# One encoder layer on one core: the first squares summed by TensorE, the first norm's factors applied early by ScalarE, a second pair of output tiles without Strassen, and new durations in the planner

## The chip, the core and the metric

The kernel runs on one core of a Trainium2 chip. The core has TensorE (PE, matmuls), VectorE (DVE), ScalarE (ACT), GpSimd (POOL) and SyncE (SP, which here starts nearly all DMAs); each takes its own instructions in order, and they wait for each other through semaphores. In the profile PE stands for matmuls and PEld for the loads of their left operand, which overlap them. The metric is device time of one execution in microseconds (us), the median of 3 runs.

## The reference

One layer of a streaming encoder on 1024 prompt tokens and 32 sample tokens, model width 1024, all in fp32:

```python
x = x + 0.5 * rmsnorm(swiglu(rmsnorm(x, g1a), f1g, f1u, f1d), g1b)
m, ... = mixer(rmsnorm(x, gma), ...)        # attention heads and a gated linear recurrence, side by side
x = x + rmsnorm(m, gmb)
x = x + 0.5 * rmsnorm(swiglu(rmsnorm(x, g2a), f2g, f2u, f2d), g2b)

def rmsnorm(x, g):  return x * rsqrt(mean(x * x, -1) + eps) * g
def swiglu(x, wg, wu, wd):  return (silu(x @ wg) * (x @ wu)) @ wd      # inner width 2816
```

Results are x, the keys and values, and the recurrence's last states.

## The kernel before

Activations lie transposed: the model width on the 128 partitions (8 blocks), the 1056 tokens along the free dimension. The tokens are cut into two sides of 528, and each side into two units of 264; the first feed-forward block takes them as four units. Each fp32 operand is split into a rounded part and a remainder (`split`, a cast on ACT or DVE and a subtraction on DVE), and a product is three matmuls (`mm3`): high by high, high by low, low by high.

`ffn` computes a SwiGLU. Its 22 blocks of inner width are taken as 11 pairs. For pair 0 the products are plain: `natural_products` makes 16 `mm3` for each unit and each of gate and up, so that a unit can start as soon as its own norm is done. From pair 1 on, `products` makes a 2 x 2 x 2 Strassen-like scheme of 7 products of 24 matmuls (168 for gate, 168 for up) in place of 8; it needs sums of blocks of W (`left_operands`) and of X (`right_operands`), which DVE makes, and split casts of them. A product that is added to two outputs is copied out of PSUM by ACT first (`p1`).

A norm is made in three steps: `square_sum` squares each block on ACT (`sq`) and adds it on DVE into `acc`; `rstd` sums `acc` over the partitions with one fp32 matmul for each 128 tokens against a column of ones (`st`), scales it on DVE (`ms`), raises it to -1/2 on POOL, and spreads it over the partitions with three matmuls against the identity (`st` again); then DVE multiplies each block by its gain and by `st` (the scalar_tensor_tensor in `start`'s `end`). In the trace each of these fp32 matmuls of `st` stands as two records.

No order is written by hand. `Planner` records every operation, replays it against a table of durations (`engine_cost`), of delays between engines (`LATENCY`) and of ScalarE's function tables (`TABLES`), tries priorities in several passes, and pins on each engine the order of the best plan; for some casts and copies (`copier`) it also picks the engine, ACT or DVE. So a changed number changes the order in the whole program, and which engine does a cast. After the first feed-forward block come the projections (`pp`), the recurrence (`recur`: matmuls `pg`, sigmoids `ig` and `lx`, tanh and square root in `th`), four attention heads (scores `Sh...`, softmax `P...`, transposes `tps...`, `oh...`), the output projection (`po`) and the second feed-forward block. All records of the trace carry one line, 142, of the planner's `call`, so the rows are told apart by tile names: `pq` for gate and up, `pd` and `pe` for down.

Of the kernel before, what the change touches and what calls it, by code (L numbers as in the profile page):

```python
# [12 lines left out]
F32 = mybir.dt.float32  # L13
# [16 lines left out]
LOUD = 0  # L30
HURRY = 2e4, 0.0, 0.0
# [17 lines left out]
class Planner:  # L49
# [142 lines left out]
    def forward(self, prio):  # L192
# [20 lines left out]
        while todo:  # L213
# [53 lines left out]
            for j, kind in self.after[i]:  # L267
                d = ops[j]
                if kind == ORDER:
                    x = start[i]  # L270
                elif op.size:
                    x = end[i]
                else:
                    x = end[i] + (0 if len(d.engines) == 1 and d.engines[0] == e and (e == "tensor" or kind == AGAIN) else LATENCY[e][d.engines[0]])
                est[j] = max(est[j], x)
                left[j] -= 1
                if not left[j]:
                    release(j)
        return chosen, start, end, order, max(end)

    def backward(self, prio, chosen):
# [12 lines left out]
        while todo:  # L294
# [19 lines left out]
            for j, kind in self.deps[i].items():  # L314
                o = ops[j]
                if kind == ORDER:
                    x = t + cost - o.cost(chosen[j])
                elif o.size:
                    x = t + cost + o.moved + 700 + o.landing
                else:  # L320
                    x = t + cost + (0 if chosen[j] == e and (e == "tensor" or kind == AGAIN) else LATENCY[chosen[j]][e])
# [43 lines left out]
    def pin(self):  # L365

        for row in self.plan.order.values():
# [9 lines left out]
           "vector": {"scalar": 130, "vector": 130, "gpsimd": 180, "sync": 130, "tensor": 256},  # L377
           "scalar": {"scalar": 145, "vector": 145, "gpsimd": 180, "sync": 145, "tensor": 270},
# [3 lines left out]
class Op:  # L382
    def __init__(self, engines, bias, name, args, kw, floor):
# [73 lines left out]
TABLES = {AF.Exp: ("exp",), AF.Tanh: ("exp", "sigmoid"), AF.Sigmoid: ("sigmoid",), AF.Sqrt: ("sqrt",),  # L457
# [3 lines left out]
def engine_cost(engine, op):  # L461
# [4 lines left out]
    if engine == "tensor":  # L466
# [25 lines left out]
def trunk(ctx: ExitStack, tc: tile.TileContext, plan, xt, w1g, w1u, w1d, w2g, w2u, w2d, win, wv, wout, kpast, vpast,  # L492
# [75 lines left out]
    def square_sum(state, src, ring):  # L568
        n = src.shape[2]
        for i in range(src.shape[1]):  # L570
# [24 lines left out]
    def rstd(stat, acc, rest=None):  # L595
        st = stat.stat.tile([128, 512], F32, "st")
        n = acc.shape[1]
# [8 lines left out]
        sums(acc, 504)  # L606
# [19 lines left out]
    def boundary(yp, acc, a, b, res, post_scale, store, then, rest=None):  # L626

        st = rstd(stat, acc, rest)
        for c in range(KD // 2):
# [3 lines left out]
            if rest is not None:  # L633
                for i in range(2):
                    act.activation(y[:, i], y[:, i], AF.Copy, scale=post_scale(2 * c + i))
                dve.tensor_mul(y, y, type(st)(st.tensor, st.offset, [st.ap[0], [0, 2], st.ap[1]]))
            for i in range(2 if rest is None else 0):
# [95 lines left out]

    def products(ps, W, X, out, up_part):


        n = 2
# [43 lines left out]
    def ffn(tails, stat, sides, wg, wu, wd, cuts, finish, last=False):  # L781
# [4 lines left out]
        def gate_up(p):  # L786
            H = [S.tile([128, 2, SB], F32, "H") for _ in range(2)]
            quarters = halves(H[0]) + halves(H[1])
            if p:
                for k, w in enumerate((wg, wu)):  # L790
                    W = left_operands([w[2 * p], w[2 * p + 1]])
                    products(stat.four, W, X, quarters, k)
# [20 lines left out]
            place.close()  # L813
            for s, _, _ in sides:
                X[s] = right_operands(Z[s], X[s])
            return H, quarters
# [121 lines left out]
        place = stat.open(2)  # L938
        for a, b in cuts:
# [6 lines left out]
            for c in range(KD // 2):  # L946
# [3 lines left out]
                for i in range(2):  # L950
# [3 lines left out]
                    if end:  # L954
                        dve.tensor_add(y[:, i], y[:, i], t)
                        square_sum(rest_ if i else acc, y[:, i:i + 1], tp)
                if not end:
                    dve.tensor_add(y, y, q[0][:, :, :b - a])
                    square_sum(acc, y, tp)
            finish(yp, acc[0], a, b, rest_[0])  # L960
# [6 lines left out]
    def start(s):  # L967
# [3 lines left out]
        def part(e):  # L971
# [8 lines left out]

            def end(Z):
# [17 lines left out]
    def finish1(yp, acc, a, b, rest):  # L999
# [5 lines left out]
        def then(c, y):  # L1005
# [3 lines left out]
            square_sum(acc2, y, tp)  # L1009
# [5 lines left out]
    ffn(three, stat, [start(0), start(1)], w1g, w1u, w1d, CUTS1, finish1)  # L1015
# [451 lines left out]
    def mixed(s):  # L1467
# [3 lines left out]
        def part(e):  # L1471
# [6 lines left out]
            def begin(Z):  # L1478
                for c in range(KD // 2):
# [5 lines left out]
                    square_sum(acc, yp(c), tp)  # L1485

            def end(Z):
                def then(c, y):
                    if y is not None:
                        square_sum(acc2, y, up)  # L1490
                        return
                    st = rstd(stat, acc2[0])
                    for c in range(KD // 2):
                        for i in range(2):
                            dve.scalar_tensor_tensor(yp(c)[:, i], yp(c)[:, i], col("g2a", 2 * c + i), st,
                                                     op0=ALU.mult, op1=ALU.mult)
# [8 lines left out]
    def finish2(yp, acc, a, b, rest):  # L1505
        boundary(yp, acc, a, b, x2_d, lambda k: half[:, 8 + k:9 + k],
                 lambda c, a, b: y_o["y%d_o" % a][:, 2 * c:2 * c + 2], lambda c, y: None, rest=rest)

    ffn(three, stat, [mixed(1), mixed(0)], w2g, w2u, w2d, CUTS, finish2, last=True)
# [81 lines left out]
```

## Time and profile before

| | |
|---|---|
| median of 3 runs | 1951.77 us (1951.39 to 1957.23) |
| profiled execution | 1959.79 us, of which the span of the trace is 1958.0 us |
| PE busy | 1897.3 us, 97% |
| DVE, ACT, POOL busy | 1417.7, 656.2, 62.2 us |
| mean granted clock of TensorE | 0.987 |

PE is the busy engine, so that time is lost where PE waits, where it runs at its lower clock, or where it is given more matmuls. Matmul records overlap: one of 264 columns lasts 0.28 us in the trace, but the next starts 0.12 us after it, so that rates are read from counts in a stretch.

### The profile page before, as it was taken

To read this page: it belongs to the slowest core of one execution; us is meant where nothing else is said; L and a number is where in the kernel's file an instruction comes from. 1 tells how busy PE (TensorE), PEld (TensorE's weight loads), DVE (VectorE), ACT (ScalarE), POOL (GpSimd) and SP (SyncE) were. 2 spreads that over 40 slices of the span, in tenths; PEclk is the share of its full clock that TensorE was granted. 3 is DMA by queue.
4 is the path that set the end of the run, shared out by engine and by line. 5 is a ranking of instruction groups with operands and counts; after the bars stand their busy time and mean duration, and the time that the engine had idled before them with its cause. 6 is when DMAs were issued, how large, how long until landed. Compare 5 with 4: busy or idle time off the path is not lost. (4 is left out here: it accounts for less than half of the span.)

```text
span 1958.0 us, 35215 instructions
## 1 busy us (share of the span) xinstructions
PE 1897.3 (97%) x14456; PEld 1853.7 (95%) x14456; DVE 1417.7 (72%) x2612; ACT 656.2 (34%) x1292; POOL 62.2 (3%) x79
## 2 busy tenths in 40 slices
PE   6999999999999999998999899999999999999997
PEld 6999999999999999897988699999999999999997
DVE  8867677675888588348677857987676666687947
ACT  5322122223232053046367753432222221333302
POOL 1000000000000010000100000100000000000000
PEclk9999999999999998999999799999999999999998
DMA  3232333324634254134434432332323323553442
GB/s 133 83 104 83 99 105 105 104 83 145 214 105 149 88 153 133 65 124 123 112 105 113 128 109 84 111 110 83 112 97 110 93 83 99 172 194 122 141 143 89
DMA packets 127810, 225.61 MB, mean 115 GB/s; under 512 B 11424, under 2 KB 84896, under 8 KB 127648
## 3 DMA queue, kind: packets, MB, share of 16 engines
q1 hardware_dynamic: 127504, 223.31, 36.0%
q8 instruction: 113, 1.85, 0.4%
q14 instruction: 49, 0.40, 0.1%
q10 hardware_dynamic: 144, 0.05, 0.0%
HBM read 157.48 MB, written 65.83 MB: 114 GB/s over the span
## 5 line engine op out<-in xcount | busy, mean ns | idle before, releaser
L142 PE MATMUL pq<-X,W 128*128 128x264 f32 x7488 | 926.8, 286 | 11.0 <-ACT p L142 4.7
L142 PEld LDWEIGHTS pq<-X,W 128*128 128x128 f32 x7488 | 921.8, 190 | 12.7 <-ACT p L142 5.1
L142 PE MATMUL pd<-T,W 128*128 128x264 f32 x3024 | 368.6, 284 | 0.0
L142 PEld LDWEIGHTS pd<-T,W 128*128 128x128 f32 x3024 | 368.1, 188 | 0.0
L142 ACT CAST W<-raw 128x512 fp32r<-128x512 f32 (+1 forms) x251 | 147.7, 601 | 433.3 <-PE pq L142 269.7
L142 DVE TENSOR_TENSOR W<-raw,W 128x512 fp32r<-128x512 f32 (+1 forms) x376 | 243.9, 669 | 5.7 <-ACT W L142 2.2
L142 DVE TENSOR_TENSOR u<-p,pq 128x528 f32<-128x528 f32 x80 | 56.3, 703 | 180.4 <-PE pq L142 180.1
L142 PE MATMUL pp<-xm,w 128*128 128x352 f32 x384 | 128.1, 334 | 6.1 <-DVE y L142 2.8
L142 PE MATMUL pp<-xm,wl 128*128 128x352 f32 x384 | 127.0, 332 | 1.9 <-DVE wl L142 1.9
L142 DVE TENSOR_TENSOR raw<-raw 128x512 f32<-128x512 f32 (+1 forms) x150 | 115.0, 771 | 17.0 <-DMA raw<-in_w2d 9.0
L142 DVE TENSOR_TENSOR u<-u,pq 128x528 f32<-128x528 f32 x80 | 56.3, 704 | 48.7 <-PE pq L142 48.4
L142 ACT CAST T<-traw 128x528 fp32r<-128x528 f32 x75 | 45.3, 633 | 118.6 <-DMA traw<-t_d 96.1
L142 DVE TENSOR_TENSOR T<-traw,T 128x528 fp32r<-128x528 f32 x126 | 84.2, 702 | 1.1
L142 PEld LDWEIGHTS pp<-xm,w 128*128 128x128 f32 x384 | 73.6, 192 | 8.3 <-ACT sq L142 3.0
L142 PE MATMUL po<-cat,w 128*128 128x264 f32 x256 | 74.9, 298 | 2.6 <-DVE y L142 1.5
L142 POOL TENSOR_TENSOR ms<-ms,neghalf 128x3 f32<-128x3 f32 x24 | 29.2, 1218 | 1518.1 <-DVE ms L142 1518.1
L142 DVE TENSOR_TENSOR acc<-acc,sq 128x264 f32<-128x264 f32 x167 | 68.9, 426 | 11.4 <-ACT sq L142 9.6
L142 PEld LDWEIGHTS pp<-xm,wl 128*128 128x128 f32 x384 | 73.7, 192 | 3.3 <-DVE wl L142 2.8
L142 PE MATMUL po<-cat,wl 128*128 128x264 f32 x256 | 72.7, 290 | 1.6 <-DVE wl L142 0.9
L142 PE MATMUL pe<-h,w 128*128 128x264 f32 x256 | 73.3, 287 | 0.0
L142 PE MATMUL pe<-hl,w 128*128 128x264 f32 x256 | 72.9, 285 | 0.0
L142 PE MATMUL pe<-h,wl 128*128 128x264 f32 x256 | 72.7, 286 | 0.0
(408 smaller groups left out, 2531.6 us busy)
## 6 DMA issues: line engine op xcount, KB each, us to landing
t_d<-H SPq DMA_DIRECT2D x126, 264.0 KB, 2.2
traw<-t_d SPq DMA_DIRECT2D x56, 528.0 KB, 4.5
raw<-in_w1g SPq DMA_DIRECT2D x22, 512.0 KB, 3.6
raw<-in_w1u SPq DMA_DIRECT2D x22, 512.0 KB, 4.1
raw<-in_w2g SPq DMA_DIRECT2D x22, 512.0 KB, 3.6
raw<-in_w2u SPq DMA_DIRECT2D x22, 512.0 KB, 3.9
raw<-in_w1d SPq DMA_DIRECT2D x36, 256.0 KB, 4.4
raw<-in_w2d SPq DMA_DIRECT2D x36, 256.0 KB, 4.3
```

The costliest lines, as they stand in the source:

```text
L142: self.made.append(f(*args, **kw).ins)
```

## The change

Four things. (1) For units 0 and 1 of the first norm (`MATRIX`), ACT squares two blocks in one instruction, and PE sums the squares over blocks and partitions: 24 fp32 matmuls of one column for each unit in place of 3, and no adds on DVE. (2) In all four units of the first norm (`SCALED`), ACT multiplies each block by its gain before the norm's factor is known (32 activations), and DVE then multiplies by `st` two blocks at a time (16 tensor_tensor in place of 32 scalar_tensor_tensor). (3) In the first feed-forward block (`PLAIN` 2) pair 1 is plain as well, by `natural_quarters`: 192 matmuls for gate and 192 for up in place of 168 and 168, and X's sums come after it. The second feed-forward block is as it was (`PLAIN` 1), and so is the end of the program (`early` holds there where `rest` was given before). (4) The planner's numbers:

```diff
-           "vector": {... "tensor": 256},
-           "scalar": {... "tensor": 270},
+           "vector": {... "tensor": 140},
+           "scalar": {... "tensor": 155},
...
+        self.tail = 280 * (name == "matmul" and self.reads[1].dtype == F32)
...
-TABLES = {AF.Exp: ("exp",), AF.Tanh: ("exp", "sigmoid"), ...
+TABLES = {AF.Exp: ("exp",), AF.Tanh: ("exp",), ...
...
-        return max(n * 4 / 2.4, 215)
+        return max(n * 2 / 2.4, 112)
...
+        if name == "tensor_tensor_scan":
+            return 69 + 2 * n / 0.96
```

The code of the other three:

```diff
+PLAIN = 2, 1
+MATRIX = "start0", "start1"
+SCALED = "start",
...
+    class Matrix:
+        def __init__(self, stat, n):
+            self.st, self.n, self.begun = stat.stat.tile([128, 512], F32, "st"), n, False
+
+        def add(self, sq):
+            for i in range(sq.shape[1]):
+                for j, a in enumerate(range(0, self.n, 128)):
+                    b = min(a + 128, self.n)
+                    pe.matmul(self.st[:, 504 + j:505 + j], sq[:, i, b - 128:b], ones[:, 0:1], start=not self.begun,
+                              stop=True, skip_group_check=True)
+                    self.begun = True
...
+    def square_sum(state, src, ring, where=None, stat=None):
         n = src.shape[2]
+        if where in MATRIX:
+            if state[0] is None:
+                state[0] = Matrix(stat, n)
...
+                sq = ring.tile([128, src.shape[1], n], F32, "sq")
+                act.activation(sq, src, AF.Square)
+                state[0].add(sq)
+            return
...
+    def scaled(ys, g, st, early):
+        if early:
+            for c, y in enumerate(ys):
+                for i in range(2):
+                    act.activation(y[:, i], y[:, i], AF.Copy, scale=g(2 * c + i))
+            st = st()
+            for y in ys:
+                dve.tensor_mul(y, y, twice(st))
+            return
...
+    def natural_quarters(ps, W, X, out, up_part):
+        for r in range(2):
+            for e in range(2):
+                t = ps.tile([128, 2, 512], F32, "pq")
+                for s in range(2):
+                    for h in range(2):
+                        for kk in range(4):
+                            a, b = X[s][h, e][kk // 2], kk % 2
+                            mm3(t[:, s, :HB], W[r, h], cslice(kk), (a[0][:, b], a[1][:, b]), slice(0, HB),
+                                h == kk == 0, h == 1 and kk == 3)
...
             if p:
                 for k, w in enumerate((wg, wu)):
-                    W = left_operands([w[2 * p], w[2 * p + 1]])
-                    products(stat.four, W, X, quarters, k)
+                    W = left_operands([w[2 * p], w[2 * p + 1]], p < plain)
+                    (natural_quarters if p < plain else products)(stat.four, W, X, quarters, k)
+                    if k and p == plain - 1:
+                        sums()
...
                 for c in range(KD // 2):
-                    square_sum(acc, z[c], tp)
-                st = rstd(stat, acc[0])
-                for c in range(KD // 2):
-                    for i in range(2):
-                        dve.scalar_tensor_tensor(z[c][:, i], z[c][:, i], col("g1a", 2 * c + i), st, op0=ALU.mult, op1=ALU.mult)
+                    square_sum(acc, z[c], up if mark in MATRIX else tp, mark, stat)
+                scaled(z, lambda k: col("g1a", k), lambda: rstd(stat, acc[0]), "start" in SCALED)
```

What the planner makes of it stands in the order of each engine. PE's first instructions, before (`st` is the norm's tile, `pq` the first products, `X` a split unit, `W` a split weight):

```order
L142 MATMUL st_450<-ones_344,acc_427 128x1 x3
L142 MATMUL st_450<-ident_348,ms_451 128x128 x2
L142 MATMUL st_450<-ident_348,ms_451 128x8
L142 MATMUL pq_480<-X_468,W_373 128x264
L142 MATMUL pq_531<-X_468,W_389 128x264
L142 MATMUL pq_480<-X_468,W_373 128x264 x5
L142 MATMUL pq_480<-X_471,W_373 128x264
L142 MATMUL st_609<-ones_344,acc_586 128x1 x3
```

and now:

```order
L145 MATMUL st_427<-ones_344,sq_444 128x1 x6
L145 MATMUL st_427<-ones_344,sq_452 128x1 x6
L145 MATMUL st_427<-ident_348,ms_468 128x128 x2
L145 MATMUL st_427<-ident_348,ms_468 128x8
L145 MATMUL st_596<-ones_344,sq_597 128x1 x6
L145 MATMUL st_596<-ones_344,sq_605 128x1 x6
L145 MATMUL st_596<-ones_344,sq_613 128x1 x6
L145 MATMUL st_596<-ones_344,sq_621 128x1 x6
L145 MATMUL pq_490<-X_478,W_373 128x264
L145 MATMUL pq_541<-X_478,W_389 128x264
L145 MATMUL pq_490<-X_478,W_373 128x264 x5
L145 MATMUL pq_490<-X_481,W_373 128x264 x2
```

All 24 sums of unit 0 (the last 12 are shown) and all 24 of unit 1 now stand ahead of the first product; before, three of unit 0 did.

ACT's instructions between the recurrence and the first head's softmax, before (`th` is first a tanh, and from itself a square root; `a2` are squares; `P` are the exponentials of head 0):

```order
L142 ACT_TABLE_LOAD
L142 ACTIVATE th_9467<-th_9467 128x1060
L142 ACTIVATE a2_9745<-lx_8641 128x352
L142 ACTIVATE th_9528<-th_9528 128x1060
L142 CAST w_10052<-raw_10051 128x1024
L142 ACTIVATE th_9650<-th_9650 128x1060
L142 ACTIVATE th_9589<-th_9589 128x1060
L142 ACT_TABLE_LOAD
L142 ACTIVATE P0h0s_10014,sm_10008<-P0h0s_10014,mn_10007 32x544
```

and now:

```order
L145 ACT_TABLE_LOAD
L145 ACTIVATE th_9499<-th_9499 128x1060
L145 ACTIVATE a2_9754<-lx_8667 128x354
L145 ACTIVATE a2_9767<-lx_8670 128x352
L145 ACT_TABLE_LOAD
L145 ACTIVATE th_9682<-lx_8673,sp8_8646 128x1060
L145 ACTIVATE lx_8673<-lx_8673,sp8_8646 128x1060
L145 ACT_TABLE_LOAD
L145 ACTIVATE th_9560<-th_9560 128x1060
L145 ACT_TABLE_LOAD
L145 ACTIVATE P0h0s_10046,sm_10040<-P0h0s_10046,mn_10039 32x544
```

The four square roots stood together and now alternate with the last tanh and the first exponentials, with a table load at each turn; two of them follow later, behind head 0's first exponentials. In the whole program ACT has 40 table loads, 33 before.

## Rows read from the trace of the kernel before

**Rows 1.** Page, busy time of PE, PEld, DVE, ACT and POOL.

```profile
PE 1897.3 (97%) x14456; PEld 1853.7 (95%) x14456; DVE 1417.7 (72%) x2612; ACT 656.2 (34%) x1292; POOL 62.2 (3%) x79
```

**Rows 2.** What PE waited for, whole program: total us, times, longest.

```profile
PE st L142 <- DVE acc L142: 9.3, 2, 9.1
PE st L142 <- POOL ms L142: 6.6, 4, 2.5
```

**Rows 3.** Timeline of PE, 8.9 to 110: start, length, instructions, wait ahead.

```profile
9.09 1.44 PE L142 MATMUL st<-ones,acc 128*128 128x1 f32 x6 [9.09 <-DVE acc L142]
13.05 1.45 PE L142 MATMUL st<-ident,ms 128*128 128x128 f32 x6 [2.52 <-POOL ms L142]
16.14 0.81 PE L142 MATMUL pq<-X,W 128*128 128x264 f32 x2 [1.65 <-ACT X L142]
19.41 1.69 PE L142 MATMUL pq<-X,W 128*128 128x264 f32 x6 [2.46 <-DVE X L142]
...
22.09 1.89 PE L142 MATMUL pq<-X,W 128*128 128x264 f32 x7
...
26.54 3.87 PE L142 MATMUL pq<-X,W 128*128 128x264 f32 x16
...
34.15 0.79 PE L142 MATMUL pq<-X,W 128*128 128x264 f32 x2
...
35.87 13.13 PE L142 MATMUL pq<-X,W 128*128 128x264 f32 x93
49.53 35.40 PE L142 MATMUL pq<-X,W 128*128 128x264 f32 x287 [0.53 <-DVE W L142]
87.19 22.99 PE L142 MATMUL pq<-X,W 128*128 128x264 f32 x174 [2.26 <-ACT p L142]
```

**Rows 4.** Timeline of PEld around the second unit's sums.

```profile
20.79 1.35 PEld L142 LDWEIGHTS st<-ones,acc 128*128 128x128 f32 x6
22.02 1.21 PEld L142 LDWEIGHTS pq<-X,W 128*128 128x128 f32 x5
```

**Rows 5.** Windows: stretch, length, PE busy and count, granted clock, DMA share, GB/s.

```profile
38.00:39.00 1.00, 1.00 (x6) 1.00 0.00 0
...
40.00:41.00 1.00, 1.00 (x11) 1.00 0.00 0
...
88.00:89.00 1.00, 1.00 (x7) 0.50 0.06 16
```

**Rows 6.** Windows: busy and count of PE, PEld, DVE, ACT, POOL; clock, DMA share.

```profile
20.00:30.00 10.00, 10.00 (x47) 9.71 (x45) 10.00 (x28) 6.85 (x17) 0.97 (x1) 1.00 0.01 4
...
905.00:935.00 30.00, 25.06 (x138) 21.34 (x136) 29.07 (x47) 13.37 (x22) 6.23 (x8) 0.94 0.36 113
...
1085.00:1125.00 40.00, 32.96 (x152) 24.93 (x151) 35.23 (x84) 28.48 (x68) 4.26 (x5) 0.74 0.41 130
```

**Rows 7.** Timeline of all engines, 0 to 20.

```profile
3.99 0.42 ACT L142 ACTIVATE acc<-x 128x264 f32<-128x264 f32 x1 [0.20 <-DMA x<-in_xt]
...
8.27 0.62 ACT L142 CAST W<-raw 128x512 fp32r<-128x512 f32 x1 [0.45 <-DMA raw<-in_w1g]
...
15.46 0.63 ACT L142 CAST X<-x 128x528 fp32r<-128x528 f32 x1 [1.03 <-DVE x L142]
```

**Rows 8.** The chain that ended last, in order of time: start, length, what.

```profile
1301.22 284.19 PE pq L142 x2319
```

**Rows 9.** Groups of DVE, 835 to 1245: busy us, mean ns, idle before.

```profile
L142 DVE CAST K<-raw 128x1056 fp32r<-128x1056 f32 x6 | 4.3, 708 | 0.5 <-DMA raw<-k_d 0.5
L142 DVE COPY pth1q<-tpsh1q 128x512 f32<-128x512 f32 x4 | 2.6, 681 | 0.0
```

**Rows 10.** Timeline of ACT in the recurrence.

```profile
862.64 1.17 ACT L142 ACTIVATE th<-lx,sp 128x1060 f32<-128x1060 f32 x1
863.83 1.28 ACT L142 ACT_TABLE_LOAD   x1
865.13 1.19 ACT L142 ACTIVATE lx<-lx,sp 128x1060 f32<-128x1060 f32 x1
```

More of the change, by code (lines that the diff above doesn't have):

```diff
@@ L273, in forward @@
                 else:
-                    x = end[i] + (0 if len(d.engines) == 1 and d.engines[0] == e and (e == "tensor" or kind == AGAIN) else LATENCY[e][d.engines[0]])
+                    x = end[i] + (0 if len(d.engines) == 1 and d.engines[0] == e and (e == "tensor" or kind == AGAIN) else LATENCY[e][d.engines[0]] + op.tail)
                 est[j] = max(est[j], x)
@@ L320, in backward @@
                 else:
-                    x = t + cost + (0 if chosen[j] == e and (e == "tensor" or kind == AGAIN) else LATENCY[chosen[j]][e])
+                    x = t + cost + (0 if chosen[j] == e and (e == "tensor" or kind == AGAIN) else LATENCY[chosen[j]][e] + o.tail)
                 est[j] = max(est[j], x)
@@ L605, in rstd @@
         m = tiny["ms"].tile([128, k])
-        sums(acc, 504)
+        if not known:
+            sums(acc, 504)
         dve.tensor_scalar(m, st[:, 504:504 + k], 1.0 / DM, EPS, op0=ALU.mult, op1=ALU.add)
@@ L624, in block, with twice, boundary @@
         return dram[s, :, 2 * c:2 * c + 2, a - s * SB:b - s * SB]
-    def boundary(yp, acc, a, b, res, post_scale, store, then, rest=None):
+    def scaled(ys, g, st, early):
[7 more added lines that the diff above has]
+            return
+        st = st()
+        for c, y in enumerate(ys):
+            for i in range(2):
+                dve.scalar_tensor_tensor(y[:, i], y[:, i], g(2 * c + i), st, op0=ALU.mult, op1=ALU.mult)
+    def twice(st):
+        return type(st)(st.tensor, st.offset, [st.ap[0], [0, 2], st.ap[1]])
+    def boundary(yp, acc, a, b, res, post_scale, store, then, rest=None, early=False):
         st = rstd(stat, acc, rest)
@@ L632, in boundary @@
             y = yp(c)
-            if rest is not None:
+            if early:
                 for i in range(2):
                     act.activation(y[:, i], y[:, i], AF.Copy, scale=post_scale(2 * c + i))
-                dve.tensor_mul(y, y, type(st)(st.tensor, st.offset, [st.ap[0], [0, 2], st.ap[1]]))
-            for i in range(2 if rest is None else 0):
+                dve.tensor_mul(y, y, twice(st))
+            for i in range(0 if early else 2):
                 dve.scalar_tensor_tensor(y[:, i], y[:, i], post_scale(2 * c + i), st, op0=ALU.mult, op1=ALU.mult)
@@ L732, in natural_products @@
                 act.activation(out[r], t[:, r, :HB], AF.Silu)
+    def natural_quarters(ps, W, X, out, up_part):
[8 more added lines that the diff above has]
+                                h == kk == 0, h == 1 and kk == 3)
+                o = out[2 * r + e]
+                if up_part:
+                    dve.tensor_mul(o, o, t[:, :, :HB])
+                else:
+                    act.activation(o, t[:, :, :HB], AF.Silu)
     def products(ps, W, X, out, up_part):
@@ L813, in gate_up, with sums @@
             place.close()
+            if plain == 1:
+                sums()
+            return H, quarters
+        def sums():
             for s, _, _ in sides:
                 X[s] = right_operands(Z[s], X[s])
-            return H, quarters
         for p in range(FF // 2):
@@ L938, in ffn @@
         place = stat.open(2)
+        mark = "end2" if last else "end1"
         for a, b in cuts:
@@ L955, in ffn @@
                         dve.tensor_add(y[:, i], y[:, i], t)
-                        square_sum(rest_ if i else acc, y[:, i:i + 1], tp)
+                        square_sum(rest_ if i and mark not in MATRIX else acc, y[:, i:i + 1], tp, mark, stat)
                 if not end:
                     dve.tensor_add(y, y, q[0][:, :, :b - a])
-                    square_sum(acc, y, tp)
-            finish(yp, acc[0], a, b, rest_[0])
+                    square_sum(acc, y, tp, mark, stat)
+            finish(yp, acc[0], a, b, rest_[0], last and (a, b) == cuts[-1])
         place.close()
@@ L997, in trunk, with finish1 @@
     xm, rbs = [], []
-    def finish1(yp, acc, a, b, rest):
+    def finish1(yp, acc, a, b, rest, end):
         if not xm:
@@ L1503, in mixed, with finish2 @@
         return s, tiles, [part(1), part(0)]
-    def finish2(yp, acc, a, b, rest):
+    def finish2(yp, acc, a, b, rest, end):
         boundary(yp, acc, a, b, x2_d, lambda k: half[:, 8 + k:9 + k],
-                 lambda c, a, b: y_o["y%d_o" % a][:, 2 * c:2 * c + 2], lambda c, y: None, rest=rest)
-    ffn(three, stat, [mixed(1), mixed(0)], w2g, w2u, w2d, CUTS, finish2, last=True)
+                 lambda c, a, b: y_o["y%d_o" % a][:, 2 * c:2 * c + 2], lambda c, y: None, rest=rest, early=end)
+    ffn(three, stat, [mixed(1), mixed(0)], w2g, w2u, w2d, CUTS, finish2, PLAIN[1], last=True)
     p3_.close()
```

36 lines of the change are left out of this document (20 added, 16 removed).

## The prediction

> **What bounds the kernel now.** The page comes first: PE is busy 1897.3 of 1958.0 us [rows 1], so PE's matmuls are the length, and what else counts is where PE waits or runs slowly. The list of waits puts the largest at the start: 9.3 us for `acc`, 6.6 us for POOL's `ms` [rows 2]. The timeline of PE says what the start is worth [rows 3]. The sums of unit 0 run at 9.09, its broadcast ends at 14.50, and up to 35.87 PE makes only 2 + 6 + 7 + 16 + 2 = 33 products, in pieces, since DVE delivers the split X piece by piece: from 20 to 30 DVE is busy 10.00 of 10 us [rows 6]. So the first stage is bound by DVE and by the norm's chain, not by PE. Then come 93 products in one piece, 0.53 us of wait, 287, and at 87.19 a wait of 2.26 us for a copy of ACT [rows 3]. In the long middle of a feed-forward block nothing waits: 2319 products take 284.19 us [rows 8], 0.1225 us each.
>
> Of the clock: 16 products from 26.54 take 3.87 us, 0.242 us each [rows 3], and at 38 a microsecond shows 6 matmuls where at 40 it shows 11 [rows 5]. That is the pace of the stretch after the wait at 87.19, where the granted clock is 0.50, the lower of the two levels, 1.2 GHz [rows 5]; at the start the column says 1.00 and the pace says otherwise. The pace rose at about 39.4, some 3.5 us after the unbroken run from 35.87 began.
>
> From 690 to 1310 the waits are small and many. Two stretches stand out: 905 to 935 (PE busy 25.06 of 30 us, clock 0.94) and 1085 to 1125 (32.96 of 40, clock 0.74); DVE is busy 29.07 and 35.23 us in them, ACT 13.37 and 28.48 [rows 6]. There DVE is the limit.
>
> **Part 1, sums by PE.** Unit 0's sums are 24 matmuls in place of 3, 48 records. Six records of loads take 22.02 - 20.79 = 1.23 us [rows 4], 0.205 each, so 48 take 9.8 us at the lower level. The first x is there at 3.99 [rows 7]; a square of 528 costs ACT about the 0.63 us of its cast of that size [rows 7], so PE begins near 4.8. The fourth x now has a weight load ahead of it in SP's queue. It lands at the latest when the first weight did, 8.27 [rows 7], long before PE gets to it, so PE itself is the limit: 4.8 + 9.8 = 14.6. From the end of the sums at 10.53 to the end of the broadcast at 14.50 were 4.0 us [rows 3]; `ms` finds DVE idle now, so I take 3.6: 18.2. The order puts unit 1's 24 sums next, 9.8 us more: first product at 28.0, where before it stood at 16.14. By then DVE, free of 14 adds and with 16 wider multiplications for 32, has split all of unit 0, so that PE no longer waits: 9 products at 0.242 (30.2), unit 1's broadcast (1.4, to 31.6), and an unbroken run. I let the clock rise 3.5 to 6.9 us later (the run from 26.54 lasted 3.87 us without a rise), 36.5 in the middle; 20 products fit before. The 67 others of unit 0 take 8.2 us at 0.1225, and the four groups of `st` of units 2 and 3 that are still to come about 0.6 each, half of 1.23: 47.1 us with 96 products done.
>
> **Part 2, factors on ACT.** 32 activations of 264 at 0.42 [rows 7] are 13.4 us more for ACT in the first 60 us. They lie beside PE's sums (ACT is busy 6.85 of 10 us from 20 to 30 [rows 6]) and I cost them at nothing. If the cover is gone, the Silu that frees the first PSUM bank comes late: up to 2 us.
>
> **Part 3, pair 1 plain.** 48 products more, 48 x 0.1225 = 5.9 us. It takes away the copy `p` and the sums of X that crowd DVE at the turn from pair 0 to 1. So the wait at 87.19 goes, and with it the slow stretch behind it: 2.26 us, and 3.4 us at half pace, 1.7; 4.0 together. What is late next would be the split W of pair 2; DVE then has all of pair 1, some 47 us of PE, for about 20 us of X's sums, so I expect no wait there.
>
> The balance at the end of pair 1. Before: 126 products done at 49.53, 594 left at 0.1225, plus 4.0: 126.3. After: 47.1 + (288 + 384) x 0.1225 = 129.4. So the first two parts nearly break even (PE's sums eat what DVE gives back) and the whole is +3.1 us, from +1 (rise of the clock at once) to +6 (late rise and a bank's wait).
>
> **Part 4, the new order of the middle.** No row shows it. By the order, DVE loses between 835 and 1245 two casts of K (0.708 each), three wide copies (0.681) [rows 9] and several smaller things, about 4.9 us together, which go to ACT; 7 table loads of 1.28 us [rows 10] come to ACT, 9.0 us. Bounds: if every wait and slow stretch of the two spots went, 29 us gained (4.94 + 1.8 and 7.04 + 10.4, by [rows 6], is 24.2, the rest smaller waits of 5); if PE stood for each new table load, 9.0 us lost. I take -3.5: seven tenths of the 4.9, since DVE is the full engine where PE waits, and none of the table loads, since ACT has room. The first feed-forward block's other pairs, its down products and the second block have the same work in nearly the same order: 0. The numbers of the planner themselves cost nothing at run time.
>
> The Trainium skill speaks against this part: ScalarE: Activation LUTs, section "What ACT_TABLE_LOAD costs", adds a drain to each load and puts a switch at 2.66 us. By that, 7 switches would be 18.6 us of ACT. The trace disagrees: the load at 863.83 starts 0.02 us after the tanh ended, and the next instruction 0.02 us after the load [rows 10].
>
> **Sum.** 3.1 - 3.5 = -0.4 us. Against the profiled execution (1959.79 us, of which 1.8 lie outside the span) that is 1959.4; that execution was 8.0 us above the median of the runs shown, 1951.77, so the forecast for the median is 1951.4 us. A change under 0.3% (5.9 us) can't be told from none here. The forecast's own range is 1946 to 1957.
>
> **Rivals.**
> A, faster: the new order takes away half of the loss at the two spots. Before, DVE's lateness at the start of a head lets PE wait, and each wait of a few us brings a stretch at the lower clock behind it; 24.2 / 2 = 12.1 us. For it: DVE is full there, and loses work. Against it: the scores still wait for the same K and Q loads and the same softmax. Time 1951.8 + 3.1 - 12.1 = 1942.8.
> B, slower: the table loads stand on the path. The square roots of the recurrence and the first exponentials of head 0 now alternate, so that ACT's exponentials, for which PE's transposes wait, come behind loads and tanh; the 4.9 us taken from DVE come to ACT as well. It decides from about 4 of the 7 loads waited for: 5.1 us, and no gain. Time 1951.8 + 3.1 + 5.1 = 1960.0. For it: ACT is already busy 28.48 of 40 us at the later spot [rows 6]. Against: ACT idles half of the earlier one.
> C, the sums lift the clock. If PE's continuous sums counted as work for the clock, the second 24 would run at half the time (4.9 us less) and the first 29 products too (29 x 0.12 = 3.5): -8.4, 1943.0. Against it stands the trace: from 20 to 30 PE was busy 10.00 of 10 us [rows 6], sums and broadcasts among the products, and the pace stayed low. It is the rule of the Trainium skill's TensorE: Matmul & The Clock Gate, section "What's actually happening", which ties the level to how busy the engine has lately been; by that rule, read plainly, C should happen, and the trace does not bear it out.
>
> **Chances and range.** Forecast 0.50; A 0.21; B 0.20; C 0.05; the rest 0.04, split. Faster by over 0.3% comes from A and C and half the crumbs, 0.27; slower from B, 0.21; within 0.3% 0.52. The range takes in B and nearly all of A and C, with the bounds of the start: 1941 to 1961.
>
> **What would show it.** In the new profile: 48 records of sums ending near 14.6 at 0.2 us each; first product near 28, not before 25 (C would show it near 23); pace 0.12 from about 36; no wait of PE between 32 and 126; the end of pair 1 near 129. If PE stands at the start of pair 2, part 3 is wrong. In the middle: fewer waits for DVE in the windows that answer to 905 to 935 and 1085 to 1125 (A), or waits for ACT's `P` and `th` (B). A first product before 20, or a loss of more than 10 us in the middle, would make the whole argument wrong.

## The result and the profile after

The changed kernel takes 1964.8 us (median of 5 executions, 1962.6 to 1968.8), the kernel before 1954.7 (5 executions, 1951.4 to 1957.2): a ratio of 1.0059 with a 95% interval of 1.0048 to 1.0071, slower by 10 us by the medians, by 11.5 by the ratio. The prediction was 1951.4, with a range from 1941 to 1961; the time lies above it. Its base was low too: in the 20 to 33 executions that stand beside each later run, the kernel before has a median of 1954.7 to 1956.3, not 1951.8.

A second trace of before was taken (`before_again`, below), since the first one's execution (1959.8) was unusually long; what follows compares with the second (1955.0). The page of the changed kernel, the row that answers to [rows 1]:

```profile
PE 1912.4 (97%) x14588; PEld 1870.1 (95%) x14588; DVE 1390.9 (71%) x2546; ACT 682.8 (35%) x1327; POOL 50.9 (3%) x79
```

PE has 132 records more (84 of sums, 48 of products), DVE 66 instructions fewer. The start, timeline of PE of the changed kernel, against [rows 3]:

```profile
5.19 10.40 PE L145 MATMUL st<-ones,sq 128*128 128x1 f32 x48 [5.19 <-ACT sq L145]
16.89 1.45 PE L145 MATMUL st<-ident,ms 128*128 128x128 f32 x6 [1.30 <-POOL ms L145]
18.20 10.38 PE L145 MATMUL st<-ones,sq 128*128 128x1 f32 x48
28.44 2.33 PE L145 MATMUL pq<-X,W 128*128 128x264 f32 x9
30.56 1.28 PE L145 MATMUL st<-ident,ms 128*128 128x128 f32 x6
31.70 6.11 PE L145 MATMUL pq<-X,W 128*128 128x264 f32 x39
...
46.95 13.24 PE L145 MATMUL pq<-X,W 128*128 128x264 f32 x107
```

and the same kernel in windows, where the pace doubles, and over the turns of the first pairs:

```profile
33.00:34.00 1.00, 1.00 (x6) 1.00 (x6) 1.00 (x3) 1.00 (x4) 0.00 (x0) 1.00 0.00 0
34.00:35.00 1.00, 1.00 (x10) 1.00 (x9) 1.00 (x3) 1.00 (x3) 0.00 (x0) 1.00 0.00 0
...
30.00:120.00 90.00, 90.00 (x727) 90.00 (x727) 64.34 (x120) 28.49 (x60) 2.58 (x3) 1.00 0.11 37
```

The start is as forecast: two blocks of 48 records, the first product at 28.4, and no wait of PE in 90 us, where the first trace of before has one of 2.26 us at 87 [rows 3]. Now the marks of the program: first and last start of the down products `pd` of the two blocks, and last `pp` of the projections, first in the second trace of before, then in the changed kernel (count: least/median/longest ns, first to last start):

```profile
L142 PE MATMUL pd<-T,W x1512: 278/284/292, 490.2 to 688.8; 128*128 128x264 f32 x189
L142 PE MATMUL pp<-xm,wl x384: 317/323/662, 735.8 to 1080.4; 128*128 128x352 f32 x192
L142 PE MATMUL pd<-T,W x1512: 278/284/293, 1700.8 to 1887.3; 128*128 128x264 f32 x189
```

```profile
L145 PE MATMUL pd<-T,W x1512: 278/284/391, 494.1 to 693.2; 128*128 128x264 f32 x189
L145 PE MATMUL pp<-xm,wl x384: 317/323/659, 740.1 to 1080.4; 128*128 128x352 f32 x192
L145 PE MATMUL pd<-T,W x1512: 278/284/296, 1708.7 to 1895.4; 128*128 128x264 f32 x189
```

The changed kernel makes the last `pd` of the first block 4.4 us late (688.8 to 693.2), has made all of it good at the last projection (1080.4 both), and then loses 7.9 us before the second block's down products (1700.8 to 1708.7). The spans differ by 8.5. So between these two traces the loss opens far behind the code that was changed; what that is worth, the experiments have to show. The windows show the place; second trace of before, then the changed kernel:

```profile
690.00:1085.00 395.00, 381.02 (x2298) 351.87 (x2296) 281.69 (x609) 198.84 (x401) 34.39 (x49) 0.98 0.40 119
1085.00:1200.00 115.00, 105.85 (x747) 96.13 (x746) 82.65 (x187) 68.06 (x178) 8.97 (x9) 0.96 0.37 122
1200.00:1330.00 130.00, 124.06 (x997) 122.35 (x996) 112.55 (x229) 50.97 (x105) 8.70 (x7) 0.99 0.29 87
```

```profile
690.00:1085.00 395.00, 382.34 (x2331) 352.29 (x2330) 282.13 (x607) 211.76 (x415) 25.73 (x49) 0.99 0.40 119
1085.00:1200.00 115.00, 107.29 (x744) 97.59 (x745) 83.78 (x188) 68.17 (x179) 8.73 (x9) 0.94 0.35 120
1200.00:1330.00 130.00, 119.66 (x939) 118.62 (x938) 110.89 (x227) 47.02 (x101) 7.19 (x7) 0.95 0.28 85
```

From 1200 to 1330 PE makes 939 matmuls where it made 997; 58 at 0.1225 us are 7.1 us. Who it waits for there, in the changed kernel, and the first of these waits in the timeline of PE:

```profile
PE st L145 <- DVE acc L145: 4.4, 1, 4.4
PE pq L145 <- ACT p L145: 2.8, 1, 2.8
PE pq L145 <- ACT X L145: 2.6, 1, 2.6
```

```profile
1212.70 0.28 PE L145 MATMUL po<-cat,wl 128*128 128x264 f32 x1
1217.35 1.41 PE L145 MATMUL st<-ones,acc 128*128 128x1 f32 x6 [4.36 <-DVE acc L145]
```

and DVE of the changed kernel in that time:

```profile
1212.18 0.43 DVE L145 TENSOR_TENSOR acc<-acc,sq 128x264 f32<-128x264 f32 x1
1212.52 0.71 DVE L145 TENSOR_TENSOR y<-y,r 128x528 f32<-128x528 f32 x1
1213.14 0.43 DVE L145 TENSOR_TENSOR acc<-acc,sq 128x264 f32<-128x264 f32 x1
...
1216.77 0.43 DVE L145 TENSOR_TENSOR acc<-acc,sq 128x264 f32<-128x264 f32 x1
```

PE came to the sums of a norm at about 1213, when DVE had made two of that norm's seven adds (the second at 1212.18) and did the others in turn with other work, the last at 1216.77; the products of `po` behind the sums, which follow at once when the sums are through, stood in the queue. The wait and the lower clock behind it (0.95 in place of 0.99 over the stretch) cost the 4.4 us and more: from 1217 to 1222 the granted clock is 0.50, the lower level. No line of this code was changed, but the planner's duration for these sums was. The long chain of [rows 8] then runs as before, 2.7 us later than in the first trace and 7.6 later than in the second (1296.35):

```profile
1303.94 283.95 PE pq L145 x2317
```

### The profile page after: what moved, and what is told of

It reads as the page before. It is cut to its first block, busy times and chain, and to the rows that moved or that the text cites. A ratio compares the mean times of both kernels' runs of the same rounds, so it can differ in the third digit from the quotient of the medians.

```text
span 1961.7 us, 35448 instructions
## 1 busy us (share of the span) xinstructions
PE 1912.4 (97%) x14588; PEld 1870.1 (95%) x14588; DVE 1390.9 (71%) x2546; ACT 682.8 (35%) x1327; POOL 50.9 (3%) x79
## 4 chain that ended last, share of the span: by engine, by line
PE 91%; DVE 4%; DMA 2%; ACT 1%; issue 1%; SPq 0%; POOLq 0%; POOL 0%; DVEq 0%; ACTq 0%
PE pq L145 45%; PE pd L145 19%; PE pp L145 8%; PE pe L145 5%; PE po L145 4%; PE pv L145 3%; PE st L145 3%; DVE y L145 1%; PE Sh1q L145 1%; PE oh2q L145 0%; PE pg L145 0%; PE Sh3q L145 0%; DVE W L145 0%; PE Sh2q L145 0%; DVE wl L145 0%
## 5 line engine op out<-in xcount | busy, mean ns | idle before, releaser
L145 ACT CAST W<-raw 128x512 fp32r<-128x512 f32 (+1 forms) x256 | 151.7, 603 | 393.5 <-PE pq L145 246.1
L145 ACT CAST T<-traw 128x528 fp32r<-128x528 f32 x85 | 51.9, 635 | 137.7 <-DMA traw<-t_d 102.6
L145 DVE TENSOR_TENSOR u<-u,pq 128x528 f32<-128x528 f32 x76 | 53.5, 704 | 46.3 <-PE pq L145 45.5
L145 DVE CAST W<-raw 128x512 fp32r<-128x512 f32 (+1 forms) x116 | 48.6, 424 | 35.0 <-PE pq L145 15.8
L145 DVE TENSOR_TENSOR acc<-acc,sq 128x264 f32<-128x264 f32 x153 | 63.9, 429 | 11.9 <-ACT sq L145 10.6
```

Source lines behind the costliest of these rows:

```text
L145: self.made.append(f(*args, **kw).ins)
```

## The experiments

T1 was the theory that the code of the first stage is the loss; T2, that the new planner numbers make a worse order in the middle and at the turn to the second block; T3, that any new order of this program is worth some us either way, whatever made it. All times are medians with the kernel before on the same chip, all ratios against it with a 95% interval.

**The kernel before, traced again** (no edit).

> The kernel before, profiled once more. The changed kernel is 10 us slower by the medians (1964.8 against 1954.7), but only 3.7 us by the two traces, since the profiled execution of before (1959.8) lay above all its others. Theory T1 (the loss is made by the start and the plain pair and is in the traces as +3.1 at the end of pair 1; the rest is the execution that happened to be profiled): this trace ends near 1951 to 1953, and what it is shorter by is spread over the program. Theory T2 (a stage with DMA waits is now longer or shorter by chance): the difference of the two traces of before sits in one stage, the middle from 690 to 1310.

1955.0 us, span 1953.2: 4.8 us shorter than the first trace. Of these, 1.5 lie before the last `pd` of the first block and 3.3 between there and the first `pd` of the second. So a single trace of this kernel is uncertain by some us, and the first was a long one. (In this expectation T1 and T2 stand for two other theories, which it states itself; the time is above the 1951 to 1953 of the first, and the difference isn't in one stage, as the second has it.)

**The code without the numbers.**

```diff
-"tensor": 140}, "tensor": 155}        (vector, scalar)
+"tensor": 256}, "tensor": 270}
-self.tail = 280 * (...)
+self.tail = 0
-AF.Tanh: ("exp",)
+AF.Tanh: ("exp", "sigmoid")
-return max(n * 2 / 2.4, 112)
+return max(n * 4 / 2.4, 215)
-if name == "tensor_tensor_scan": return 69 + 2 * n / 0.96
```

> Sums by PE, factors on ACT and the plain pair 1, but with the planner's numbers of before. T1 (the code of the first stage is the loss): 1962 to 1966, as the changed kernel, with the end of pair 1 some 3 us late. T2 (the new numbers make a worse order in the middle and at the turn to the second block): 1955 to 1959, only the 3 us of the first stage. T3 (any new order of this program differs by several us either way): anything from 1950 to 1968, with waits at other places than in the changed kernel.

1964.3 us, 1.0046 (1.0032 to 1.0060). The time is T1's, but the way there is another: the last `pd` of the first block comes at 704.0, not 693.5, since PE stands 4.89 us in the first pair and then runs at the lower level (granted clock 0.50 from 75 to 79). PE, then ACT, of this kernel:

```profile
75.12 0.59 PE L145 MATMUL pq<-X,W 128*128 128x264 f32 x1 [4.89 <-ACT H L145]
```

```profile
73.87 0.63 ACT L145 CAST X<-x 128x528 fp32r<-128x528 f32 x1 [19.86 <-DVE W L145]
74.41 0.67 ACT L145 ACTIVATE H<-pq 128x264 f32<-128x264 f32 x2
```

A cast of X stands ahead of the Silu that frees PSUM, and waits for DVE; PE waits for the Silu. Later stages give all of it back against the changed kernel: 382.7 us from that `pd` to the last `pp` against 387.3, and 621.7 from there to the first `pd` of the second block against 628.0.

**The numbers without the code.**

```diff
-PLAIN = 2, 1;  MATRIX = "start0", "start1";  SCALED = "start",
+PLAIN = 1, 1;  MATRIX = ();  SCALED = ()
```

> The code of before with the planner's new numbers (latencies, matmul cost and tail, tanh's table, scan). T1: within 2 us of before, 1953 to 1957. T2: slower by 6 to 8 us, 1961 to 1963, with the waits of the turn to the second block (4.4 us for acc, 2.6 for X, 2.8 for p in the changed kernel). T3: anything from 1950 to 1968.

1954.6 us, 0.9993 (0.9981 to 1.0006). T2's 6 to 8 us are not there: in this order the numbers alone move nothing that can be measured. By the spread of the orders below, one order is weak evidence on an effect of that size.

**The changed kernel with the old start** (`MATRIX = ()`, `SCALED = ()`).

> The changed kernel without sums by PE and without the factors on ACT: plain pair 1 and new numbers stay. By the prediction's parts 1 and 2 the start is even (96 products done at 47.1 against 96 + 30 at 49.5, that is +1.3 us for the sums): 1963 to 1965, the same as the changed kernel within 2 us. If the sums by PE are the loss: 1955 to 1959. T3: anything from 1950 to 1968.

1960.0 us, 1.0023 (1.0014 to 1.0033): between the two expectations. The last `pd` of the first block is at 691.8, 1.7 earlier than in the changed kernel; the rest of the 4.8 us between the medians lies in the later stages.

**The changed kernel with pair 1 as before** (`PLAIN = 1, 1`).

> The changed kernel, but pair 1 by the Strassen-like products as before (sums by PE, factors on ACT and the new numbers stay). Theory P (the 48 more products cost their 5.9 us and what they save, the stall behind pair 0, is worth less): 5.9 us less work and a stall of 2 to 4 us back, as in the kernel with the numbers alone, where PE stands 1.36 + 0.63 + 1.26 us between 56 and 96: 1961 to 1963. If the plain pair pays for itself, as the prediction had it to within 2 us: 1964 to 1967.

1956.1 us, 1.0003 (0.9995 to 1.0012), below both expectations: 8.7 us faster than the changed kernel by the medians, 11 by the ratios, more than the 5.9 us of products that it saves. At the last `pd` of the first block only 3.0 of them are there (690.5 for 693.5). Taken alone, this run would have been read as a price of 8.7 us for the plain pair; that reading doesn't hold, as the next runs show.

**The changed kernel with DVE's adds, factors still on ACT** (`MATRIX = ()`).

> The changed kernel, but with the squares of units 0 and 1 added by DVE as before; factors on ACT, plain pair 1 and new numbers stay. Without both parts the time was 1960.0. Theory M (the 48 matmuls of one column, 20.8 us of PE at the start, are the start's cost): 1958 to 1961, the 96th product near 42.4. Theory S (the factors on ACT are the cost, since ACT is late with the rest): 1963 to 1966, the 96th product near 45.

1960.5 us, 1.0021 (1.0013 to 1.0030). The time is Theory M's, but the way there is neither theory's: the 96th product ends at 36.6 us, before both 42.4 and 45, and 9.3 us are then lost in two waits for `H`, the first for a Silu of ACT, with the lower level between and behind them (0.50 from 72 to 77):

```profile
66.14 1.47 PE L145 MATMUL pq<-X,W 128*128 128x264 f32 x5 [4.77 <-ACT H L145]
72.12 3.23 PE L145 MATMUL pq<-X,W 128*128 128x264 f32 x13 [4.51 <-DVE H L145]
```

The last `pd` of the first block is at 692.0, where the changed kernel has 693.5, but the two marks can't be compared: 47 of the block's 384 `pe` matmuls start ahead of it here, 96 in each other trace, and 49 at 0.1225 us are 6.0 us. The last `pe` ends at 738.5, in the changed kernel at 734.8, in the one with the old start at 733.9. So with the factors on ACT the sums by PE don't cost time in the first block, they save 3.7 us; the factors alone, against the old start, bring the two waits and 4.6 us. All this is one order of each.

**A number moved by 2 ns.**

```diff
-LATENCY = {"tensor": {"scalar": 200, "vector": 198, ...
+LATENCY = {"tensor": {"scalar": 200, "vector": 200, ...
```

> The kernel before with one number of the planner moved by 2 ns (delay from TensorE to VectorE 198 to 200), which no row could tell, but which makes other orders of all engines. Theory T3 (each new order of the middle and of the turn to the second block is worth some us by itself, either way): off from 1954.7 by 2 us or more, with stage lengths that differ by 2 to 5 us in the projections, heads and turn. Theory T1 (such orders are alike to about 1 us): 1953.5 to 1956.

1951.5 us, 0.9978 (0.9968 to 0.9988): faster than before by more than the interval. T3 is borne out: a number that no row could tell is worth 4 us.

**The numbers without the short delays** (256 and 270 stay; code of before).

> The code of before with the new numbers except the two delays towards TensorE (256 and 270 stay). From the end of po to the first pd of the second block the three kernels with all new numbers took 456.3, 455.8 and 455.9 us, those with the old ones 452.9, 452.8 and 453.3. If the short delays make that loss (X is planned to be ready before it is): 453 in that stretch and 1950 to 1953 in all. If the halved matmul cost makes it: 456 in that stretch and 1953 to 1956 in all.

1953.1 us, 0.9983 (0.9975 to 0.9992). The stretch from `po` to `pd` is 448.2, below both expectations; and the kernel with pair 1 as before, which has the short delays, has 453.4. The delays are not the cause. The wait of 4.37 us for `acc` at 1217 stands here as well, and the last `pd` of the first block is at 693.9, where the numbers with the short delays have 688.4 and the changed kernel 693.5, though the code is that of before.

**Two other draws of the changed kernel** (198 to 200, 198 to 196).

> The changed kernel with the same number of the planner moved by 2 ns as in the nudged kernel before (TensorE to VectorE 198 to 200). In the changed kernel the stretch from the last pp (1080.8) to the first pd of the second block (1708.7) lasts 628.0 us, in nine other traces 613.8 to 622.1. Theory T3 (that stretch is a draw of the planner, not a consequence of the change): it comes to 614 to 622 here, with other stalls, and the time to 1955 to 1962. Theory D (the changed code and numbers lead there each time): 626 to 630, the stall of about 4.4 us for acc near 1217 again, and 1963 to 1967.

> As the one before, with 196 in place of 200: a second draw. T3: 614 to 622 in that stretch and 1955 to 1962. D: 626 to 630 and 1963 to 1967. What both theories keep: the end of the first block's down products pd near 693.5 (+3 to +5 against before), since it rests on counted matmuls.

1956.0 us, 0.9999 (0.9991 to 1.0008), and 1956.0 us, 1.0006 (0.9997 to 1.0015). D falls: with 2 ns more or less the changed kernel is as fast as before. From the last `pp` to the first `pd` it takes 616.8 and 618.0 us in place of 628.0. What PE waits for from 1200 to 1330, with 200:

```profile
PE st L145 <- DVE acc L145: 2.2, 2, 1.2
PE pq L145 <- ACT W L145: 0.7, 1, 0.7
PE pq L145 <- ACT X L145: 0.4, 1, 0.4
```

3.3 us where the three largest of the changed kernel make 9.8, and waits at other places.

**The changed kernel with the old duration of fp32 matmuls** (215 and no tail).

> The changed kernel with the planner's old duration for fp32 matmuls and without the tail (latencies, tanh's table and scan stay new). The stall for acc of 4.4 us stands in the changed kernel and in the one with the new numbers but old latencies, 2.1 us in the one with the new numbers alone, and in none with the old duration. Theory N (the halved duration lets the planner put the sums of a norm too early on TensorE): no wait for acc above 1 us between 1190 and 1260, and 1957 to 1961. T3: a draw like the others, 1955 to 1966, with or without that wait.

1964.7 us, 1.0051 (1.0038 to 1.0064). The wait for `acc` is gone, as Theory N has it, and the stretch from the last `pp` is the shortest of all (611.4), but the time isn't Theory N's: the last `pd` of the first block is at 704.4, since PE again stands for a Silu (3.70 us at 76.6), as in the code without the numbers. In both kernels with the new code and the old duration this stall stands, in all six traces with the new code's sums and the new duration it doesn't. So this number seems to help the changed start, by some 10 us.

On the wait itself Theory N fares better than this one run: from 1185 to 1340 PE waits over 2 us for `acc` in 5 of the 10 traces with the new duration (of either code) and at most 1.1 us in the 8 with the old. All its waits there are alike, though: 2.5 to 11.5 us, 5.7 on the average, with the new duration, and 1.1 to 9.0, 5.0 on the average, with the old. So the new number probably brings this wait, but no loss of the stretch is shown from it.

**Before with 196.**

> The kernel before with TensorE to VectorE at 196. The nudge to 200 gave 1951.5 against 1956.3 (ratio 0.9978). T3: another draw, between 1949 and 1960, the stretch from the last pp to the first pd between 613 and 623 where before has 620 to 622. If the nudge to 200 was a real correction (a longer delay is nearer to the chip): this one is as before or slower, 1954 to 1960.

1964.9 us, 1.0053 (1.0040 to 1.0066): as slow as the changed kernel, without any of the change, and slower than either theory expected. The stretch from the last `pp` lasts 630.1 us, above the 613 to 623; its trace is of the longest execution of six (1970.5). Its waits from 1200 to 1330 and its windows there and ahead of it:

```profile
PE po L142 <- DVE y L142: 2.7, 1, 2.7
PE pq L142 <- ACT X L142: 2.6, 1, 2.6
PE st L142 <- POOL ms L142: 1.8, 1, 1.8
```

```profile
1085.00:1200.00 115.00, 104.31 (x717) 93.70 (x717) 83.45 (x194) 67.38 (x172) 10.59 (x10) 0.96 0.37 117
1200.00:1330.00 130.00, 121.85 (x930) 119.92 (x929) 109.17 (x226) 50.13 (x107) 9.31 (x7) 0.93 0.31 92
```

930 matmuls from 1200 to 1330, close to the 939 of the changed kernel, with other waits.

**Two more draws of each** (199 and 202).

> The kernel before, another draw (199 ns in place of 198). Draws so far: 1955.6, 1951.5, 1964.9. T3: anywhere from 1950 to 1966; the first pd of the second block comes 1005 to 1026 us after the last pd of the first. What no draw should move: that last pd of the first block, at 686 to 691.

> The kernel before with 202 ns. T3: anywhere from 1950 to 1966, the last pd of the first block at 686 to 691.

> The changed kernel, another draw (199 ns). Draws so far: 1964.8, 1956.0, 1956.0. The last pd of the first block should stand at 692 to 698 in every draw, some 5 us behind before's, since 48 matmuls and the sums are counted work. If the change costs its 5 us on the average: the mean of the two new draws is above that of before's two by 3 to 7. If the later stages take it back, as the prediction's -3.5 says: within 2.

> The changed kernel with 202 ns: as the one before, 1952 to 1966, the last pd of the first block at 692 to 698.

1961.3, 1947.4, 1970.4 and 1958.8 us. The marks of the first block came as expected, the times did not: 1947.4 and 1970.4 lie outside their ranges, and the two new draws of the changed kernel are 10 us above the two of before by their means, where 3 to 7 or under 2 was expected.

The ten draws together (marks from one trace each, in us; before with 198 by its second trace):

| ns | before: ratio | last `pd`, block 1 | to first `pd`, block 2 | after: ratio | last `pd`, block 1 | to first `pd`, block 2 |
|---|---|---|---|---|---|---|
| 196 | 1.0053 (1.0040 to 1.0066) | 690.7 | 1025.0 | 1.0006 (0.9997 to 1.0015) | 696.9 | 1006.9 |
| 198 | 1 | 689.1 | 1011.7 | 1.0059 (1.0048 to 1.0071) | 693.5 | 1015.3 |
| 199 | 1.0032 (1.0020 to 1.0045) | 689.2 | 1017.4 | 1.0082 (1.0068 to 1.0097) | 692.2 | 1020.2 |
| 200 | 0.9978 (0.9968 to 0.9988) | 686.8 | 1007.8 | 0.9999 (0.9991 to 1.0008) | 693.8 | 1009.2 |
| 202 | 0.9967 (0.9955 to 0.9980) | 690.1 | 1002.6 | 1.0018 (1.0009 to 1.0028) | 695.7 | 1009.6 |
| mean | 1.0006 | 689.2 | 1012.9 | 1.0033 | 694.4 | 1012.2 |

The mark at the end of the first block parts the two kernels in every draw: 686.8 to 690.7 before, 692.2 to 696.9 after, 5.2 us by the means. A draw moves it too, by 4 or 5 us, and the old code with the numbers and old delays (693.9) lies among the changed kernels; with five draws of each the standard error of the 5.2 is 1.1. The stretch behind it doesn't part them: it spreads over 22 and 13 us, and its means are 0.7 apart, with a standard error of 4.6. The ratios differ by 0.27%, 5.2 us, with a standard error of 0.23% from the spread (0.36% in each row of five). So the change has a cost of about 5 us that stands in the first block, shown by the marks, and nothing shows the rest of the 10 us to be more than the draw; that the total cost is above nothing is likely but not shown by the ratios alone. Two draws of before (200 and 202) are faster than before itself, and with 202 it takes 1947.4 us, the fastest of all here: the kernel that beats both is the old code with a lucky order.

## Why the prediction was wrong, point by point

**What bounds it.** Right: PE is busy 97%, and every us of the result is a wait, a lower clock or a count of matmuls.

**Part 1.** Right to about a us up to the first product, by two misses that cancel: the 48 records took 10.40 us, not 9.8, so that the sums, begun at 5.19 (4.8 forecast), end at 15.6 (14.6), but the chain from there to the end of the broadcast took 2.75 us, not 3.6, and ends at 18.3 (18.2). The first product starts at 28.4 (28.0). The pace rose at 34, not 36.5 and before the earliest time that the prediction allowed (3.5 us after 31.6), so 96 products were done at 45.7, not 47.1.

**Part 2.** Right for this order: from 30 to 120 PE never waits, so ACT's 32 factors are covered. Without the sums by PE they were not (the wait of 4.77 us above).

**Part 3.** Right in what happens: the stall behind pair 0 is gone, nothing took its place at pair 2, and the products are there. What it was to save, 4.0 us, was read from one trace, as the next point says.

**The balance, +3.1 (from +1 to +6).** It was stated for the end of pair 1, and there it held, by two errors that cancel in part. The 720th product of gate and up (the 768th with the plain pair) ends at 128.3 in the changed kernel and at 124.3 in the second trace of before, and at 128.5 and 124.7 by the means of the five draws: +3.8, with a standard error of 0.9. The start was put 1.7 too dear: by the means 96 products are done at 46.3 before and at 45.9 after, where the prediction's sums have 45.9 and 47.1. The rest was put 2.3 too cheap: from the 96th product to the end of pair 1 the changed kernel takes 82.6 us in every draw, before 77.6, 79.5, 77.6, 76.5 and 80.8 (196 to 202, mean 78.4). So against before 1.7 of the 5.9 us of added products came back on the average, not 4.0. The 4.0 belong to some executions only: the draw with 202 has the wait and the slow stretch behind it, the second trace of before has the wait alone, and the draw with 200 has neither; second trace, then the draw with 200:

```profile
86.60 43.68 PE L142 MATMUL pq<-X,W 128*128 128x264 f32 x356 [2.26 <-ACT p L142]
```

```profile
43.75 86.46 PE L142 MATMUL pq<-X,W 128*128 128x264 f32 x705
```

From there to the last `pd` the changed kernel takes 1.5 us more (566.0 for 564.5 by the means, standard error 0.4), where the prediction has 0; 0 to 1.6 us of it are waits for DVE's `u`. That makes the 5.2. What the plain pair costs by itself isn't settled: in the three kernels with the new numbers and pair 1 as before, the stretch from the 96th product to the end of pair 1 takes 80.6 to 82.8 us.

**Part 4, -3.5.** From the last `pd` to the last `pp` the changed kernel did take 4.4 less, but this doesn't show the prediction's reason: the same stretch is 386.4 to 403.4 us in the draws of before (in the longest, 42 more matmuls of other tiles stand ahead of the last `pp`) and 387.3 to 392.4 in those of the changed kernel. The means, 394.1 and 390.2, differ by 3.9 with a standard error of 2.9: a gain of the forecast's size is neither shown nor excluded. In the windows of [rows 6], against the second trace of before, the first spot improved and the second didn't; before, then the changed kernel:

```profile
905.00:935.00 30.00, 24.96 (x139) 21.04 (x137) 28.94 (x49) 12.45 (x22) 6.70 (x9) 0.94 0.31 93
1085.00:1125.00 40.00, 32.32 (x170) 24.71 (x169) 36.19 (x80) 29.50 (x74) 4.16 (x4) 0.87 0.34 116
```

```profile
905.00:935.00 30.00, 27.14 (x159) 23.43 (x158) 29.87 (x56) 22.25 (x33) 2.44 (x5) 1.00 0.34 114
1085.00:1125.00 40.00, 32.52 (x168) 25.35 (x169) 34.81 (x78) 29.26 (x74) 3.39 (x4) 0.83 0.33 115
```

**The step that failed** is the zero behind it, "the second block have the same work in nearly the same order: 0", taken without a spread. The stretch from the last `pp` to the first `pd` of the second block lost 7.9 us: PE's waits in it are 18.6 us against 15.2, with one new wait and two longer ones, and its granted clock is 0.978 against 0.989. The work is the same; its order is not, because every number re-orders the whole program, and this stretch came out between 613.8 and 630.1 us in the draws of before, 616.8 and 629.8 in those of the changed kernel (means 618.8 and 622.1, standard error of the difference 4.1). The prediction had bounds for the order only in the middle, where it saw idle time, and its one loss there was the table loads; an order that is drawn anew can also lose where it lost nothing before. The term should have been 0 with a spread: the standard deviation of a draw is 0.36%, 7 us. With +3.1 on the prediction's base that puts one standard deviation at 1962 and two at 1969.

**The base.** Three executions gave 1951.8, twenty and more gave about 1955: 3 us of the miss of 13.

**The rivals.** A didn't come: one spot of two, and no gain in time. B came close in time (1960.0) and is wrong in its mechanism: ACT has its 40 table loads, but PE's waits for ACT from 735 to 1200 are 2.0 us in all, 3.9 in the second trace of before. The group in the changed kernel:

```profile
L145 ACT ACT_TABLE_LOAD x40 | 51.3, 1283 | 3.4 <-PEq L1644 1.2 <-issue 0.6 <-DVE sm L145 0.5
```

Each still takes 1283 ns, and they are covered. C didn't come: with sums ahead of them, 9 products still take 2.33 us at 28.4, the lower pace, and the second 24 sums take 10.38 us, the first 10.40. (The prediction's share for faster doesn't add up as it says: 0.21, 0.05 and half of 0.04 are 0.28, not 0.27.)

Left open: tanh's table and the scan's duration were not tried by themselves, nor the factors on ACT without the plain pair and the new numbers. Each part was undone in one order only, so the runs that undo a part don't price it within the spread of a draw.

## What to carry to other kernels

Where a planner or a scheduler orders the program, a change of code is two changes: the work that can be counted, and a new draw of the order everywhere, also far from the edit. Measure the second before judging the first: move a number that means nothing, a few times, in both kernels; here the ratios lay between 0.9967 and 1.0082, with a standard deviation (0.36%) above what the change itself is worth (0.27%). Compare marks at the end of the stage that was edited, which a draw moved by 4 or 5 us here and the stretch behind it by 13 to 22, and not the total alone; and count the instructions ahead of a mark, since an order can also move what stands there. Look for a stall that a change is to remove in a second trace and a second order first: here it was in some and not in others.

## What the runs showed of the hardware

The clock at the start: in the changed kernel PE was busy without a gap from 16.89, with one-column sums and broadcasts up to 28.44; 9 products from there took 2.33 us, the pace of the lower level, and the pace doubled at 34, when products had run unbroken from 31.70. The granted clock reads 1.00 all the time, as before [rows 5], but the trace's first record of the clock stands at 34.2 us, 39.4 in the first trace of before: ahead of it the 1.00 means that nothing was recorded, and the pace has to be read from counts. In the second trace of before, the same program in the same order, the first record stands at 31.1, and the clock fell again at 34.5, after PE had stood 1.62 us up to 33.37. So the moment of the rise differs between two executions of one program by 8 us.

A single trace can mislead: the same kernel's executions lay between 1951.2 and 1960.3 us, and two traces of it differ by 4.8 us of span, 3.3 of them in stages with many short waits.
